# A transformer block on one core: a first pool of 160 bytes on the right side, and one padded tile

## The chip, the cores and the metric

The kernel runs on one core of a Trainium2 chip. The metric is the device time of one execution in microseconds (us); less is better. A profile of one execution stands beside the times. It names the engines PE (matrix multiply, with PEld for its weight loads), DVE (vector), ACT (scalar), POOL (GpSimd) and SP (which issues most DMAs).

## What is computed

One layer on a sequence of 1024 rows of 1024 numbers in float32: a SwiGLU feed-forward network (FFN), a mixer whose first half is attention with forget gates (8 heads) and whose second half is a gated linear recurrence (RG-LRU), and a second FFN. After each comes a layer norm over a scaled residual.

```python
x = layer_norm(DN_ALPHA * x + 0.5 * swiglu(x, ffn1_w_gate, ffn1_w_up, ffn1_w_down), ln1_g, ln1_b)
z = x @ w_in                                    # q, k, v, LRU input, LRU gate, forget logits
fox = forgetting_attention(q, k, v, fg)         # softmax(q k / 8 + cum_t - cum_s) v, causal
rec = rg_lru(causal_depthwise_conv(z_lx), ...)  # h_t = a_t h_(t-1) + b_t
mix = concat([fox, gelu(z_lg) * rec]) @ w_out
x = layer_norm(DN_ALPHA * x + mix, ln2_g, ln2_b)
x = layer_norm(DN_ALPHA * x + 0.5 * swiglu(x, ffn2_w_gate, ffn2_w_up, ffn2_w_down), ln3_g, ln3_b)

def swiglu(x, w_gate, w_up, w_down):
    return (silu(x @ w_gate) * (x @ w_up)) @ w_down      # 1024 -> 4096 -> 1024
```

## The kernel before

**Products.** Each float32 operand is split into a high part and a low part (ACT copies the high part, DVE subtracts it for the low part), and each product is three matmuls: `mm3`, lines 148 to 150, high by high, high by low, low by high. A matmul has a stationary operand (`lhs`, 128 columns, loaded into the array beforehand) and a moving one (`rhs`, up to 512 columns, streamed through). In `mm(out, lhs, rhs)` the profile prints the moving tile first: `b<-As,ws` has the moving tile `As` and the stationary tile `ws`.

**Stages.** The work runs in six stages one after the other, and PE's order is the order of the code:

1. `gate_up`, first FFN (up to about 659 us). Strassen-Winograd: each 2 by 2 block product is seven products instead of eight. There are 16 pairs of column blocks, with a gate and an up matrix each, so 32 matrices. A matrix is 7 products of 12 matmuls, 84 in all, in the order `one` (block A11), `two` (A12), `five`, `six`, `three`, `seven` (the sums s1, s2, s4, s3 of blocks), `four` (block A22). The moving tiles are the blocks of the activations; the stationary ones are the weights in the pool `gu_ws`, 16 buffers, refilled by ACT and DVE (lines 290 and 291). The profile leaves numbers out of names: `A` is A11, A12 and A22, `As` is the four sums.
2. `down_ffn`, first FFN (to about 980 us): seven products again, both operands from the pool `dn_ws`.
3. `mixer_in` (to about 1227 us): projections of the transposed rows `xT` by `w`, for each of four column groups and two halves 48 matmuls for the LRU and 48 for q and k, six small gate products of the LRU between them, and the v projection.
4. `attention` (to about 1456 us), with the output projection by `w_out` filled in between.
5. `gate_up`, second FFN (to about 2099 us).
6. `down_ffn`, second FFN (to the end).

**Where tiles lie.** A pool takes its room in SBUF when it is opened and gives it back when it is closed: one stack grows from the left (low addresses), one from the right (`side="right"`, high addresses). The address of each tile follows from the sizes of what was opened before it on its side. The left stack begins with the pool `const`. The right stack is empty until a stage opens `xl`, `dn_v`, `dn_w`, `att_qk`, `xr` or the second `gu_ws` there. All of the tiles that PE reads in lines 148 to 150 have sizes that are multiples of 256 bytes, so that a pool's place modulo 256 bytes holds for all its tiles. The tile `zx` of the LRU (line 597), 515 numbers long, is one that isn't.

Of the kernel before, what the change touches and what calls it, by code (L numbers as in the profile page):

```python
# [9 lines left out]
F32 = mybir.dt.float32  # L10
# [7 lines left out]
P = 128  # L18
# [5 lines left out]
H = 512  # L24
# [16 lines left out]
}  # L41
GELU_C = math.sqrt(2.0 / math.pi)


def f32(ap):
    return ap.bitcast(F32)


class Block:
    def __init__(self, ctx, tc):  # L50
        self.tc, self.nc, self.ctx = tc, tc.nc, ctx
        self.n = 0
        self.A, self.xT = {}, {}

        def pool(name, bufs=1, **kw):
            return ctx.enter_context(tc.tile_pool(name=name, bufs=bufs, **kw))

        self.const = pool("const")
        self.rawp = pool("rawp", 2)
        self.rowp = pool("rowp", NT)  # L60
        self.small = pool("small", 4)
        self.dram = pool("scr", 1, space=DRAM)
        nc = self.nc
        self.ident = self.const.tile([P, P], F32, name="ident")
        make_identity(nc, self.ident)
        self.eps = self.const.tile([P, 1], F32, name="eps")
        nc.vector.memset(self.eps, EPS)

    @contextmanager
    def pool(self, name, bufs=1, **kw):  # L70
        with self.tc.tile_pool(name=self.nm(name), bufs=bufs, reuse_waits="tile", **kw) as p:
            yield p
# [517 lines left out]
    def lru(self, c, half, s, tp, mix, state, between):  # L590

        nc, v = self.nc, self.nc.vector

        def tmp(tag, shape=(P, H), dt=F32):
            return tp.tile(list(shape), dt, tag=tag, name=self.nm(tag))

        zx = tp.tile([P, H + 3], F32, tag="zx", name=self.nm("zx"))
        if half == 0:
            v.memset(zx[:, 0:3], 0.0)
        else:  # L600
            v.tensor_copy(zx[:, 0:3], state["z"])
        nc.scalar.copy(zx[:, 3:], s[:, 0, :])
        if half == 0:
            state["z"] = self.small.tile([P, 3], F32, tag="zc", name=self.nm("zc"))
            v.tensor_copy(state["z"], zx[:, H:H + 3])
        u = tmp("u")
        v.tensor_scalar(u, zx[:, 3:], self.cw[:, c, 3:4], self.cb[:, c:c + 1], op0=ALU.mult, op1=ALU.add)
        for k in (2, 1, 0):
            v.scalar_tensor_tensor(u, zx[:, k:k + H], self.cw[:, c, k:k + 1], u, op0=ALU.mult, op1=ALU.add)
        uh, ul = tmp("ua", dt=F32R), tmp("ue", dt=F32R)  # L610
        nc.scalar.copy(uh, u)
        v.tensor_tensor(ul, u, f32(uh), ALU.subtract)
        g = tmp("g")
        nc.scalar.activation(g, s[:, 1, :], AF.Square)
        nc.gpsimd.tensor_scalar(g, g, 0.044715, 1.0, op0=ALU.mult, op1=ALU.add)
        v.tensor_tensor(g, g, s[:, 1, :], ALU.mult)
        nc.scalar.activation(g, g, AF.Tanh, scale=GELU_C)
        v.scalar_tensor_tensor(g, g, 1.0, s[:, 1, :], op0=ALU.add, op1=ALU.mult)
        between()
        gates = []  # L620
        for n in range(2):
            pa = self.a_tile()
            self.mm3(pa, tuple(w[:, n, :] for w in state["w"]), (uh, ul), True, True)
            gates.append(pa)
        t, tg, a, e = tmp("t"), tmp("tg"), tmp("ua"), tmp("ue")
        nc.scalar.activation(t, gates[0], AF.Tanh, bias=self.hba[:, c:c + 1], scale=0.5)
        nc.scalar.activation(tg, gates[1], AF.Tanh, bias=self.hbx[:, c:c + 1], scale=0.5)
        nc.scalar.activation(a, t, AF.Exp, bias=self.spm4[:, c:c + 1], scale=self.spm4[:, c:c + 1])
        nc.scalar.activation(t, t, AF.Tanh, bias=self.sp2[:, c:c + 1], scale=self.sp2[:, c:c + 1])
        v.tensor_scalar(a, a, 0.5, 0.5, op0=ALU.mult, op1=ALU.add)  # L630
        v.scalar_tensor_tensor(e, t, 1.0, a, op0=ALU.add, op1=ALU.mult)
        v.scalar_tensor_tensor(e, e, 2.0, a, op0=ALU.subtract, op1=ALU.mult)
        v.scalar_tensor_tensor(a, t, 1.0, e, op0=ALU.subtract, op1=ALU.mult)
        v.scalar_tensor_tensor(tg, tg, 1.0, u, op0=ALU.add, op1=ALU.mult)
        v.tensor_tensor(tg, tg, e, ALU.mult)
        nc.scalar.activation(t, t, AF.Sqrt)
        v.tensor_tensor(tg, tg, t, ALU.mult)
        v.tensor_tensor_scan(e, a, tg, 0.0 if half == 0 else state["h"], ALU.mult, ALU.add)
        if half == 0:
            state["h"] = self.small.tile([P, 1], F32, tag="hc", name=self.nm("hc"))  # L640
            v.tensor_copy(state["h"], e[:, H - 1:H])
        v.scalar_tensor_tensor(g, g, -0.5, e, op0=ALU.mult, op1=ALU.mult)
        hs = slice(half * H, (half + 1) * H)
        nc.scalar.copy(mix[0][:, hs], g)
        v.tensor_tensor(mix[1][:, hs], g, f32(mix[0][:, hs]), ALU.subtract)

    def forget(self):

        nc, v, c, z = self.nc, self.nc.vector, self.const, self.fgz
        l1p = self.log1p_exp_neg_abs(c, z, [P, HEADS, NT])  # L650
        v.scalar_tensor_tensor(z, z, 0.0, l1p, op0=ALU.min, op1=ALU.subtract)
        pre = l1p
        v.memset(pre[:, :, 0], 0.0)
        for i in range(1, NT):
            v.tensor_tensor(pre[:, :, i], pre[:, :, i - 1], z[:, :, i - 1], ALU.add)
        z, pre = (t.rearrange("p h i -> p (h i)") for t in (z, pre))
        n = HEADS * NT
        pc = self.a_tile()
        nc.tensor.matmul(pc[:, 0:n], self.tri, z, start=True, stop=False)
        nc.tensor.matmul(pc[:, 0:n], self.ones, pre, start=False, stop=True)  # L660
        v.tensor_copy(z, pc[:, 0:n])
        pt = self.a_tile()
        nc.tensor.transpose(pt[0:n, 0:P], z, self.ident)
        ct = c.tile([n, P], F32, name="ct")
        v.tensor_copy(ct, pt[0:n, 0:P])
        self.cum_d = self.dram.tile([HEADS, T], F32, name="cum_d")
        nc.sync.dma_start(self.cum_d.rearrange("h (i t) -> (h i) t", t=P), ct)
# [358 lines left out]
```

## Time and profile before

| | us |
|---|---|
| median of three runs | 2425.64 (2425.54 to 2429.72) |
| the profiled execution | 2431.77 |
| its span, first to last instruction | 2430.1 |
| PE busy in it | 2350.8 (97%) |
| DVE, ACT, POOL busy | 1816.1 (75%), 993.9 (41%), 384.3 (16%) |

The busy time of PE counts each matmul from its start to its modelled end. In a stream each starts before the one ahead has ended, so a matmul's length in the tables (some 390 ns) is more than the time from one start to the next (some 230 ns). The second is what a matmul costs in a stream; it is read from the start times of the timeline or from the count in a window. A shorter mean in a group's row goes with a shorter step.

### The profile page before, as it was taken

The page shows a single profiled execution, that of the slowest core. Times are in us where ns is not written, and L with a number is a line of the kernel's source. Part 1 is how long each engine was busy: PE and PEld are TensorE (multiplying, and loading weights), DVE is VectorE, ACT ScalarE, POOL GpSimd, SP SyncE. Part 2 cuts the span into 40 slices and gives each one's busy share as a digit, 9 for nine tenths or more (in the row PEclk, how much of TensorE's full clock was granted, in tenths as well). Part 3 has the DMA queues.
Part 4 walks back from the last instruction along what each step waited for, and adds up shares of the span by engine and source line. Part 5 has one row for each costly group of instructions (what it writes and reads, how often), then busy time and mean ns, then how long its engine had stood idle before and what let it go on. Part 6 is the DMA issues. An engine that isn't in the chain of part 4 may idle for free.

```text
span 2430.1 us, 29276 instructions
## 1 busy us (share of the span) xinstructions
PE 2350.8 (97%) x10709; PEld 1930.3 (79%) x10709; DVE 1816.1 (75%) x3059; ACT 993.9 (41%) x1748; POOL 384.3 (16%) x461
## 2 busy tenths in 40 slices
PE   7999999999999998999999898999999999999996
PEld 5888888888888887788888677888888888788885
DVE  7877777777667878866657789776777777568878
ACT  5343333333344444543546755333333333344443
POOL 2020000000010005311134442000000000010015
PEclk8999999999999999999999998999999999999998
DMA  3333232322374442332365812332323232564342
GB/s 132 112 92 113 83 113 94 118 94 102 117 258 171 154 158 70 89 105 88 105 182 142 232 53 74 109 108 88 113 83 115 97 114 98 187 222 169 129 153 87
DMA packets 175775, 298.99 MB, mean 123 GB/s; under 512 B 8128, under 2 KB 100608, under 8 KB 175632
## 3 DMA queue, kind: packets, MB, share of 16 engines
q1 hardware_dynamic: 151984, 216.06, 27.9%
q0 software_dynamic: 23648, 81.07, 8.9%
q8 instruction: 85, 1.39, 0.3%
q14 instruction: 58, 0.48, 0.1%
HBM read 214.22 MB, written 82.87 MB: 122 GB/s over the span
## 4 chain that ended last, share of the span: by engine, by line
PE 85%; DVE 9%; issue 4%; POOL 1%; DMA 1%; ACT 1%; SPq 0%; POOLq 0%; DVEq 0%; ACTq 0%
PE b L149 17%; PE b L150 17%; PE b L148 17%; PE s L150 5%; PE s L149 5%; PE s L148 5%; PE a L150 5%; PE a L149 5%; PE a L148 5%; DVE ws L461 2%; DVE row L189 1%; PE a L846 1%; PE a L830 1%; DVE st L185 1%; DMA raw<-in_ffn_w_gate_dram 1%
## 5 line engine op out<-in xcount | busy, mean ns | idle before, releaser
L148 PE MATMUL b<-As,ws 128*128 128x512 f32 x1024 | 406.2, 397 | 7.9 <-ACT As L239 7.9
L149 PE MATMUL b<-As,ws 128*128 128x512 f32 x1024 | 407.5, 398 | 4.0 <-DVE As L240 4.0
L150 PE MATMUL b<-As,ws 128*128 128x512 f32 x1024 | 408.8, 399 | 0.0
L148 PE MATMUL b<-A,ws 128*128 128x512 f32 x768 | 300.3, 391 | 4.3 <-ACT ws L290 4.3
L149 PE MATMUL b<-A,ws 128*128 128x512 f32 x768 | 300.4, 391 | 0.0
L150 PE MATMUL b<-A,ws 128*128 128x512 f32 x768 | 299.6, 390 | 0.0
L290 ACT CAST ws<-t 128x512 fp32r<-128x512 f32 x256 | 159.2, 622 | 341.9 <-PE b L149 316.4
L460 ACT CAST ws<-raw 128x512 fp32r<-128x512 f32 x224 | 139.3, 622 | 314.8 <-PE a L150 140.6
L461 DVE TENSOR_TENSOR ws<-raw,ws 128x512 fp32r<-128x512 f32 x224 | 167.2, 747 | 119.3 <-ACT ws L460 119.2
L148 PEld LDWEIGHTS b<-As,ws 128*128 128x128 f32 x1024 | 193.6, 189 | 54.6 <-ACT As L239 8.4
L149 PEld LDWEIGHTS b<-As,ws 128*128 128x128 f32 x1024 | 193.8, 189 | 53.0 <-DVE As L240 5.2
L150 PEld LDWEIGHTS b<-As,ws 128*128 128x128 f32 x1024 | 193.9, 189 | 46.3
L290 ACT CAST ws<-raw 128x512 fp32r<-128x512 f32 x192 | 118.8, 620 | 264.2 <-PE b L149 258.6
L291 DVE TENSOR_TENSOR ws<-t,ws 128x512 fp32r<-128x512 f32 x256 | 177.9, 695 | 53.6 <-ACT ws L290 53.5
L149 PE MATMUL a<-ws,ws 128*128 128x512 f32 x512 | 202.5, 395 | 7.0 <-DVE ws L461 6.9
L148 PE MATMUL a<-ws,ws 128*128 128x512 f32 x512 | 202.2, 396 | 1.4 <-ACT ws L460 1.3
L150 PE MATMUL a<-ws,ws 128*128 128x512 f32 x512 | 202.1, 395 | 0.0
L291 DVE TENSOR_TENSOR ws<-raw,ws 128x512 fp32r<-128x512 f32 x192 | 137.0, 714 | 48.9 <-ACT ws L290 48.7
L148 PEld LDWEIGHTS b<-A,ws 128*128 128x128 f32 x768 | 144.2, 188 | 35.9 <-ACT ws L290 4.7
L424 POOL DMA_DIRECT2D h_d<-row x32 | 18.6, 582 | 960.1 <-DVE row L416 927.9
L149 PEld LDWEIGHTS b<-A,ws 128*128 128x128 f32 x768 | 144.3, 188 | 31.2
L150 PEld LDWEIGHTS b<-A,ws 128*128 128x128 f32 x768 | 144.2, 188 | 30.7
(224 smaller groups left out, 4697.8 us busy)
## 6 DMA issues: line engine op xcount, KB each, us to landing
raw<-h_d SPq DMA_DIRECT2D x56, 1024.0 KB, 5.5
h_d<-row POOLq DMA_DIRECT2D x96, 512.0 KB, 3.4
raw<-in_ffn_w_gate_dram SPq DMA_DIRECT2D x32, 1024.0 KB, 5.4
raw<-in_ffn_w_up_dram SPq DMA_DIRECT2D x32, 1024.0 KB, 5.4
wd<-in_ffn_w_down_dram SPq DMA_DIRECT2D x32, 1024.0 KB, 7.7
h_d<-row POOLq DMA_DIRECT2D x32, 256.0 KB, 4.5
raw<-in_w_in_dram SPq DMA_DIRECT2D x16, 512.0 KB, 5.2
row<-in_x_dram SPq DMA_DIRECT2D x12, 512.0 KB, 7.5
```

The costliest lines, as they stand in the source:

```text
L148: mm(out, ah, bh, start=first, stop=False)
L149: mm(out, ah, bl, start=False, stop=False)
L150: mm(out, al, bh, start=False, stop=last)
L185: v.bn_stats(st[:, j, :], a[:, j * H:(j + 1) * H])
L189: v.scalar_tensor_tensor(a, a, mv[:, 0:1], gb[0], op0=ALU.subtract, op1=ALU.mult)
L290: nc.scalar.copy(hi, src)
L291: v.tensor_tensor(lo, src, f32(hi), ALU.subtract)
L424: return nc.gpsimd.dma_start(d[:, 6], s5)
L460: nc.scalar.copy(hi, src)
L461: self.mark = v.tensor_tensor(lo, src, f32(hi), ALU.subtract)
L830: nc.tensor.transpose(pa[:, (j % 4) * P:(j % 4 + 1) * P], p[:, j * P:(j + 1) * P], self.ident)
L846: mm(pv[:, ps], vt[:, j, :], pts[h, qt][j // 4][l][:, j % 4, ps], start=j == 0 and l == 0, stop=j == last and l == 1)
```

## The change

A pool `edge` is opened first on the right side with one tile of 40 numbers (160 bytes) for each partition. No instruction touches it. All that is later opened on the right side lies 160 bytes lower. The tile `zx` is 576 numbers long instead of 515, of which 515 are used, so that what follows it in its pool and the pools after it start elsewhere. The tile `ct` of `forget` is no more; its values go into the first 64 partitions of `ones`, which was read for the last time by a product a few lines earlier. So `const` is 512 bytes smaller, and all that follows on the left lies 512 bytes lower.

```diff
+LINE = 64
+EDGE = 40
...
+        self.edge = pool("edge", side="right")
+        self.edge.tile([P, EDGE], F32, name="edge")
         self.const = pool("const")
...
-        zx = tp.tile([P, H + 3], F32, tag="zx", name=self.nm("zx"))
+        zx = tp.tile([P, H + LINE], F32, tag="zx", name=self.nm("zx"))[:, 0:H + 3]
...
-        ct = c.tile([n, P], F32, name="ct")
+        ct = self.ones[0:n]
         v.tensor_copy(ct, pt[0:n, 0:P])
```

Every engine issues the same instructions with the same shapes in the same order. The addresses that the program gives to the two operands, modulo 256 bytes:

| matmuls | count | moving, stationary before | moving, stationary after |
|---|---|---|---|
| `gate_up` 1, sums `As` (right) by `ws` | 1536 | 224, 64 | 64, 64 |
| `gate_up` 1, blocks A11, A12, A22 by `ws` | 1152 | 64, 64 | 64, 64 |
| `down_ffn` 1 and 2, `ws` by `ws` | 2688 | 64, 64 | 64, 64 |
| `mixer_in`, `xT` (right) by `w` | 768 | 224, 64 | 64, 64 |
| `mixer_in`, LRU gates, `ua`, `ue` by the gate weights | 48 | 96, 96 | 64, 64 |
| `mixer_in`, v: `wv` (0, 64, 128, 192 past 64) by `xT` | 384 | mixed, 224 | mixed, 64 |
| attention, `kh`, `kl` by `q` (all right) | 192 | 224, 224 | 64, 64 |
| attention, `pt` by `v` (right) | 320 | 64, 224 | 64, 64 |
| output projection, `w` by `mix` | 384 | 64, 64 | 64, 64 |
| `gate_up` 2, sums `As` (left) by `ws` (right) | 1536 | 64, 224 | 64, 64 |
| `gate_up` 2, blocks A11, A12, A22 by `ws` (all right) | 1152 | 224, 224 | 64, 64 |

The transposes (`ident` by a tile, line 234 and line 830) have 128 and 64 before and after.

One wait of the second `down_ffn` moves with the addresses: the DMA that loads its first `wd` tile no longer waits for PE, and the next `wd` load, two issues later on SP, does.

## The prediction

> **What bounds the kernel now.** I read the page first, then a table of windows by stage, then the list of waits, then single starts in the timeline.
>
> ```profile
> span 2430.1 us, 29276 instructions
> PE 2350.8 (97%) x10709; PEld 1930.3 (79%) x10709; DVE 1816.1 (75%) x3059; ACT 993.9 (41%) x1748; POOL 384.3 (16%) x461
> PE 85%; DVE 9%; issue 4%; POOL 1%; DMA 1%; ACT 1%; SPq 0%; POOLq 0%; DVEq 0%; ACTq 0%
> ```
>
> PE is busy for 97% of the span, and the chain that ended last runs over PE for 85% of it. A shorter matmul therefore shortens the end, as long as the matmul stands in a stretch where PE doesn't wait. The table of windows tells which stretches those are (the columns are the window, its length, busy time of PE, PEld, DVE, ACT and POOL with counts, PE's granted clock, DMA share and GB/s):
>
> ```profile
> 100.00:640.00 540.00, 540.00 (x2334) 438.54 (x2333) 395.61 (x643) 184.51 (x308) 48.33 (x73) 1.00 0.30 101
> ...
> 740.00:900.00 160.00, 160.00 (x708) 132.48 (x707) 133.60 (x209) 67.17 (x118) 6.30 (x5) 1.00 0.48 170
> ...
> 1010.00:1230.00 220.00, 217.94 (x1116) 183.62 (x1116) 138.45 (x256) 103.41 (x166) 39.13 (x60) 1.00 0.35 109
> 1230.00:1440.00 210.00, 193.78 (x1136) 164.65 (x1136) 161.05 (x415) 133.38 (x299) 89.85 (x146) 0.98 0.56 153
> ...
> 1500.00:2080.00 580.00, 580.00 (x2506) 471.01 (x2505) 427.89 (x679) 197.41 (x330) 42.34 (x61) 1.00 0.30 101
> ```
>
> In both `gate_up` stages (the first and the last row) PE is busy without a break, at the full granted clock, with DVE at 73% and 74%. In `mixer_in` it misses 2 of 220 us, in attention 16 of 210. The same rows give what a matmul costs: 540 us / 2334 = 231.4 ns in the first `gate_up`, but 160 us / 708 = 226.0 ns in `down_ffn`, although both consist of matmuls of one shape at one clock. The groups by line show where the difference is (after the bar: busy us, mean ns of one, idle us):
>
> ```profile
> L150 PE MATMUL b<-As,ws 128*128 128x512 f32 x1024 | 408.8, 399 | 0.0
> L150 PE MATMUL b<-A,ws 128*128 128x512 f32 x768 | 299.6, 390 | 0.0
> L150 PE MATMUL s<-ws,ws 128*128 128x512 f32 x384 | 149.4, 389 | 0.0
> L150 PE MATMUL s<-xT,w 128*128 128x512 f32 x256 | 101.5, 397 | 0.0
> ```
>
> Two groups are at 389 to 390 ns and two at 397 to 399. Set beside the table of addresses in the section on the change, the longer ones (`As`, `xT`) are those whose two operands differ modulo 256 bytes, and the shorter ones (`A`, `ws` by `ws`) those where they agree. The step from start to start is measured in the timeline (start, length, engine, line). First one matrix of the first `gate_up`, then one of the second, then `down_ffn`, then `mixer_in`:
>
> ```profile
> 461.83 0.39 PE L148 MATMUL b<-A,ws 128*128 128x512 f32 x1
> ...
> 463.92 0.39 PE L148 MATMUL b<-A,ws 128*128 128x512 f32 x1
> ...
> 464.60 0.39 PE L148 MATMUL b<-A,ws 128*128 128x512 f32 x1
> ...
> 470.04 0.40 PE L148 MATMUL b<-As,ws 128*128 128x512 f32 x1
> ...
> 481.28 0.39 PE L148 MATMUL b<-A,ws 128*128 128x512 f32 x1
> ...
> 1804.97 0.40 PE L148 MATMUL b<-A,ws 128*128 128x512 f32 x1
> ...
> 1813.17 0.40 PE L148 MATMUL b<-As,ws 128*128 128x512 f32 x1
> ...
> 1824.39 0.40 PE L148 MATMUL b<-A,ws 128*128 128x512 f32 x1
> ...
> 2199.66 0.39 PE L148 MATMUL a<-ws,ws 128*128 128x512 f32 x1
> ...
> 2219.38 0.39 PE L148 MATMUL a<-ws,ws 128*128 128x512 f32 x1
> ...
> 1036.22 0.40 PE L150 MATMUL a<-ua,lo 128*128 128x512 f32 x1
> ...
> 1058.95 0.40 PE L148 MATMUL a<-ua,hi 128*128 128x512 f32 x1
> ```
>
> - 464.60 to 470.04 are the products `one` and `two` (A11, A12), 24 matmuls: 5.44 / 24 = 226.7 ns.
> - 470.04 to 481.28 are the four products on sums, 48 matmuls: 11.24 / 48 = 234.2 ns. In the second `gate_up` 1813.17 to 1824.39: 11.22 / 48 = 233.8 ns. There the sums lie on the left and `ws` on the right, the other way round from the first, and the blocks A11, A12 and A22 lie on the right beside `ws`. So neither the side nor the distance sorts the groups; the difference modulo 256 does.
> - 2199.66 to 2219.38 is `ws` by `ws`, 87 steps: 226.7 ns, with both operands in a third pool.
> - 1036.22 to 1058.95 holds one gate matmul and 96 of `xT`: 22.73 / 97 = 234.3 ns.
> - 461.83 to 464.60 is `four` (A22), 12 matmuls: 2.77 / 12 = 230.8 ns, though its operands agree. The first nine take 2.09 us (232 ns each), the last three 0.68 us (227 ns). I read this as a lag that the stretch before leaves behind and that dies out within nine matmuls; the 24 after it show nothing of it.
>
> [...]
>
> **The sum.** No instruction is added, removed or moved, so the sum has the step alone.
>
> - `gate_up`, first FFN: a matrix now takes 481.28 - 461.83 = 19.45 us for its 84 matmuls. With all operands at 64 it should take 84 x 0.2267 = 19.04 us (the A22 lag goes too, because nothing before it differs). 0.41 us x 32 matrices = 13.1 us.
> - `gate_up`, second FFN: 1824.39 - 1804.97 = 19.42 us, 0.38 us x 32 = 12.2 us.
> - `mixer_in`: 768 matmuls on `xT` x (234.3 - 226.7) = 5.8 us.
> - `down_ffn`, output projection: operands agree before and after. Nothing.
> - Attention: `pt` by `v` comes to agree. I have no such matmul with equal places to price it by. If its step shrank by the same share (7.5 of 234.2, 3.2%), the group below would give at most 3.2% of 41.7 us, 1.3 us; if other work sets the pace there, as the 16 us that PE misses suggest, nothing. The v projection in `mixer_in` has three of four places still unequal. I take nothing, and keep 0 to 1.5 us for the range.
>
> ```profile
> L846 PE MATMUL a<-pt,v 128*128 128x256 f32 x256 | 41.7, 297 | 1.1 <-DVE pt L835 0.9
> ```
>
> What could hold the gain back in `gate_up` is the making of weights. The waits say who is ahead (waiting instruction, what it waited for, total us, times, longest us):
>
> ```profile
> ACT ws L290 <- PE b L149: 575.1, 349, 2.2
> ```
>
> ACT waits 575 us in all for PE to release a `ws` buffer: the weights are ready a full pool ahead, and a PE that is 2% faster only shortens these waits. DVE would go from 73% to 75%. Nor do DVE and ACT depend on where tiles lie: the same subtraction costs as much with `ws` at 64 (window 100 to 640) as with `ws` at 224 (window 1510 to 2080).
>
> ```profile
> L291 DVE TENSOR_TENSOR ws<-t,ws 128x512 fp32r<-128x512 f32 x111 | 76.0, 685 | 24.6 <-ACT ws L290 24.6
> L291 DVE TENSOR_TENSOR ws<-t,ws 128x512 fp32r<-128x512 f32 x118 | 80.8, 685 | 27.0 <-ACT ws L290 27.0
> ```
>
> The other edits cost nothing. `edge` is never touched; `zx` is read and written over the same 515 numbers; the copy into `ones` comes after a product and a transpose for which it waits anyway. The `wd` load that takes over the wait for PE is two issues behind the one that had it, so SP is free of it earlier, not later; if its cover is gone, it costs at most one landing once.
>
> Sum: 13.1 + 12.2 + 5.8 = 31.1 us. The profiled execution, 2431.77 us with a span of 2430.1, would come to 2400.7; it is 6.1 us over the median of the runs, from which I subtract: 2425.6 - 31.1 = 2394.5 us. The difference that a measurement here can tell from none is about 0.2%, 4.9 us.
>
> **Rivals.**
>
> - *Agreement alone isn't enough.* The equal products of A22 stand at 230.8 ns, not at 226.7. If that is their own pace and no lag, because something besides the remainder counts, then the sums may come down only to 230.8. Then 3072 matmuls gain 3.4 or 3.0 ns and `xT` 768 x 3.5 ns: 9.8 + 2.7 = 12.5 us, 2413 us. For it: the A22 rows. Against it: the last three of twelve are at 227.
> - *The change does nothing.* The sums and `xT` take longer for another reason that goes with these tiles, and 31 us stay: 2425.6 us. For it: only two tiles take longer, and the trace itself doesn't show the places. [...] Against it: the sums change sides between the FFNs and stay at 234, and A22 in the same stage and of the same shape settles.
> - *Equal places collide.* The remainder counts the other way: two streams that start at one remainder ask for the same thing at the same time, and something else, such as the order in which pools were filled, makes A11, A12 and `ws` quicker. A22 would then show the price of equality, 230.8 - 226.7 = 4.1 ns, to be added to the 3840 matmuls that come to agree: 15.7 us, 2441 us. It decides from the point where a sum takes over 234.2 ns in the new layout. Against it: 226.7 ns in three pools with equal places.
>
> **How the numbers follow.** The full gain has 0.78: five places agree with it and none of the 227 ns groups contradicts. The partial gain has 0.10, no effect 0.08, collision 0.04. Faster by over 0.2% holds the first two, 0.88; within it 0.08; slower 0.04. The full gain alone would be 2390 to 2399: 1.5 us more from attention and, since the shown runs are up to 4.1 us apart, about 3 us to either side. To cover a gain that is partly lost, most of the way to the partial rival, the range goes from 2389 to 2411.
>
> **What would show it right or wrong.** In the profile after, the groups `b<-As,ws` and `s<-xT,w` should have the 389 to 390 ns of the others; 48 products on sums should take 10.9 us, a block of 84 should take 19.04, and A22 should be at 227 from its first matmul. A window of 540 us in `gate_up` should hold some 2380 matmuls instead of 2334, still busy without a break, and ACT's 575 us of waiting for PE should shrink by about the 25 us. If the groups stay at 397 to 399, the remainder isn't the cause; if they fall but the span doesn't follow, another engine has become late, and `ws` L290 or L291 would then stand as what PE waits for. A lasting pace over 227 in all would speak for the partial rival.

## The result, and the profile after

| | before | after |
|---|---|---|
| median of the runs, us | 2425.8 (2425.54 to 2429.72) | 2396.19 (2391.57 to 2396.48) |
| the profiled execution, us | 2431.77 | 2396.48 |
| its span, us | 2430.1 | 2394.8 |

The ratio is 0.987, with a 95% interval from 0.9853 to 0.9887: 29.6 us less by the medians, where 31.1 were forecast. Both kernels, measured once more later, gave 2396.51 (2393.51 to 2397.09) against 2427.15 for the kernel before, ratio 0.9868 (0.9853 to 0.9883). One run of the experiment with the right side at 0 took 2530.62 us at a granted clock of 0.88, where its others had 0.986 to 0.988, and is not among that experiment's numbers below.

The head of the page of the kernel after: the instruction counts of every engine are those of before, and only PE has become shorter by more than 3 us, by 2350.8 - 2318.7 = 32.1 us.

```profile
span 2394.8 us, 29276 instructions
PE 2318.7 (97%) x10709; PEld 1927.6 (80%) x10709; DVE 1814.8 (76%) x3059; ACT 993.3 (41%) x1748; POOL 383.0 (16%) x461
PE 85%; DVE 8%; issue 3%; DMA 1%; ACT 1%; POOL 1%; SPq 0%; POOLq 0%; DVEq 0%; ACTq 0%
```

Its table of windows, one row for the first `gate_up` with the window of the prediction, and one for the second (columns as in the prediction):

```profile
100.00:640.00 540.00, 540.00 (x2384) 447.15 (x2383) 398.25 (x647) 186.96 (x313) 48.69 (x73) 1.00 0.30 103
...
1500.00:2060.00 560.00, 560.00 (x2472) 463.88 (x2471) 408.39 (x648) 192.77 (x323) 39.10 (x58) 1.00 0.31 107
```

PE is still busy without a break, with 2384 matmuls in the 540 us that held 2334 before: 226.5 ns each. The groups by line (`mm3` is at lines 153 to 155 now):

```profile
L155 PE MATMUL b<-As,ws 128*128 128x512 f32 x1024 | 400.3, 391 | 0.0
L155 PE MATMUL b<-A,ws 128*128 128x512 f32 x768 | 299.0, 389 | 0.0
L155 PE MATMUL s<-ws,ws 128*128 128x512 f32 x384 | 149.4, 389 | 0.0
L155 PE MATMUL s<-xT,w 128*128 128x512 f32 x256 | 100.2, 391 | 0.0
...
L851 PE MATMUL a<-pt,v 128*128 128x256 f32 x256 | 41.0, 294 | 1.1 <-DVE pt L840 0.9
```

`As` fell from 399 to 391 ns and `xT` from 397 to 391. `A` and `ws` by `ws`, whose operands agreed before, stayed within 1 ns. The timeline of the kernel after, at the rows where the moving tile changes, in the first `gate_up`, then the second, then `mixer_in` (start, length, engine, line):

```profile
442.49 0.39 PE L153 MATMUL b<-As,ws 128*128 128x512 f32 x1
...
453.37 0.39 PE L153 MATMUL b<-A,ws 128*128 128x512 f32 x1
...
456.08 0.39 PE L153 MATMUL b<-A,ws 128*128 128x512 f32 x1
...
461.52 0.39 PE L153 MATMUL b<-As,ws 128*128 128x512 f32 x1
...
1783.78 0.39 PE L153 MATMUL b<-As,ws 128*128 128x512 f32 x1
...
1794.66 0.39 PE L153 MATMUL b<-A,ws 128*128 128x512 f32 x1
...
1802.82 0.39 PE L153 MATMUL b<-As,ws 128*128 128x512 f32 x1
...
1023.67 0.39 PE L153 MATMUL s<-xT,w 128*128 128x512 f32 x1
...
1045.43 0.39 PE L153 MATMUL a<-ua,hi 128*128 128x512 f32 x1
```

The 48 products on sums take 453.37 - 442.49 = 10.88 us in the first FFN and 10.88 in the second (11.24 and 11.22 before). A block of 84 takes 461.52 - 442.49 = 19.03 us (19.45 before). The 12 of A22, from 453.37 to 456.08, take 2.71 us, 226 ns each. The 96 of `xT` take 21.76 us, 226.7 ns each.

Since one execution of the kernel before ran 3.7 us longer than another, the stages are set out for two profiled executions of each kernel (second pair: the same addresses, profiled again). A stage goes from its first matmul to the first one of the next, read from the start times (the 17 to 18 us ahead of the first matmul are left out):

| us | before | before again | after | after again | forecast |
|---|---|---|---|---|---|
| `gate_up` 1 | 641.30 | 641.60 | 628.95 | 629.11 | -13.1 |
| `down_ffn` 1 | 322.64 | 322.64 | 322.61 | 322.61 | 0 |
| `mixer_in` | 256.30 | 258.40 | 251.11 | 251.58 | -5.8 |
| attention | 217.83 | 214.16 | 212.93 | 212.05 | 0 to -1.5 |
| `gate_up` 2 | 643.10 | 641.10 | 630.81 | 631.11 | -12.2 |
| `down_ffn` 2 and the end | 331.13 | 331.07 | 330.83 | 330.89 | 0 |
| span | 2430.1 | 2426.4 | 2394.8 | 2394.6 | -31.1 |

The two spans of before differ by 3.7 us, and attention alone differs by as much (217.83 and 214.16). So the 35.3 us between the first two profiles is more than the change brings; the second pair differs by 31.8.

### The profile page after: what moved, and what is told of

Its sections match the earlier page's. It is cut to its first block, busy times and chain, and to the rows that moved or that the text cites. A ratio compares the mean times of both kernels' runs of the same rounds, so it can differ in the third digit from the quotient of the medians.

```text
span 2394.8 us, 29276 instructions
## 1 busy us (share of the span) xinstructions
PE 2318.7 (97%) x10709; PEld 1927.6 (80%) x10709; DVE 1814.8 (76%) x3059; ACT 993.3 (41%) x1748; POOL 383.0 (16%) x461
## 4 chain that ended last, share of the span: by engine, by line
PE 85%; DVE 8%; issue 3%; DMA 1%; ACT 1%; POOL 1%; SPq 0%; POOLq 0%; DVEq 0%; ACTq 0%
PE b L154 17%; PE b L155 17%; PE b L153 17%; PE s L155 5%; PE s L154 5%; PE s L153 5%; PE a L155 5%; PE a L154 5%; PE a L153 5%; DVE ws L466 2%; DVE row L194 2%; PE a L851 1%; DMA raw<-in_ffn_w_gate_dram 1%; DVE st L190 1%; PE a L835 1%
## 5 line engine op out<-in xcount | busy, mean ns | idle before, releaser
L153 PE MATMUL b<-As,ws 128*128 128x512 f32 x1024 | 400.7, 392 | 8.2 <-ACT As L244 8.2
L154 PE MATMUL b<-As,ws 128*128 128x512 f32 x1024 | 400.7, 391 | 3.8 <-DVE As L245 3.8
L155 PE MATMUL b<-As,ws 128*128 128x512 f32 x1024 | 400.3, 391 | 0.0
```

The source lines that it names most:

```text
L153: mm(out, ah, bh, start=first, stop=False)
L154: mm(out, ah, bl, start=False, stop=False)
L155: mm(out, al, bh, start=False, stop=last)
```

## The experiments

The theory: in a stream of 512-column matmuls of this kernel, the step from start to start depends on where the two operands lie modulo 256 bytes; equal places give 226.7 ns, others more. Its rivals: the time comes from something else in the new layout (the padded `zx`, the shorter `const`, another order of tiles); or one particular place is good, and the operands needn't agree; or two streams merely mustn't start close to each other.

### The other two edits alone

The pool `edge` is left out, and the padded `zx` and the reuse of `ones` stay. The right side is back at 224.

```diff
-        self.edge = pool("edge", side="right")
-        self.edge.tile([P, EDGE], F32, name="edge")
```

> The change without the pool on the right: zx padded and ct put into ones, so the left side lies 512 bytes lower and the right side where it was. Theory 'difference modulo 256': As and xT still differ by 160 or 96 bytes, the time stays at that of before, 2425.6 us (within 3 us), As at 234 ns a step. Rival 'the smaller const pool or the new place on the left brings it': 2396 us.

Measured: 2427.53 us (2426.3 to 2433.15) against 2427.56 (2423.2 to 2433.49), ratio 1.0 (0.9991 to 1.0009). The groups by line are those of before:

```profile
L153 PE MATMUL b<-As,ws 128*128 128x512 f32 x1024 | 408.1, 399 | 0.0
...
L153 PE MATMUL b<-A,ws 128*128 128x512 f32 x768 | 299.9, 390 | 0.0
...
L153 PE MATMUL s<-xT,w 128*128 128x512 f32 x256 | 101.8, 398 | 0.0
```

From start to start the sums of the first `gate_up` take 234.2 ns and `xT` 234.2, as before. The whole gain hangs on the 160 bytes. That is still no proof of agreement: every tile on the right moved with them.

### The right side at 192: it moves, but doesn't agree

```diff
-EDGE = 40
+EDGE = 72
```

288 bytes instead of 160: the right side lies at 192, the left at 64, and the two differ by 128.

> The pool on the right has 288 bytes instead of 160: the right side lies at 192, the left at 64, a difference of 128 everywhere. Theory 'difference modulo 256': As and xT take 231 to 238 ns a step and the time is that of before, 2420 to 2430 us. Rival 'modulo 128 or 64 is enough': 2396 us. Rival 'any shift of the right side does it': 2396 us.

Measured: 2422.54 us (2419.05 to 2427.99), ratio 0.998 (0.997 to 0.9991). From the groups by line:

```profile
L155 PE MATMUL b<-As,ws 128*128 128x512 f32 x1024 | 406.4, 397 | 0.0
...
L155 PE MATMUL s<-xT,w 128*128 128x512 f32 x256 | 101.7, 397 | 0.0
```

The steps of `As` and `xT` are 233.2 to 233.5 ns, and A22 behind them is at 228 in place of 230 to 231. A pool ahead of all others on the right is thus worth almost nothing as long as the places differ: 5 us of the 31. The steps account for that: a block of 84 takes 19.37 us in both FFNs (19.45 and 19.41 before), and `xT` 1.0 ns less, 0.08 x 32 + 0.04 x 32 + 0.8 = 4.6 us.

### Both sides at 128: they agree, elsewhere

```diff
-EDGE = 40
+EDGE = 24
...
+        self.lead = pool("lead")
+        self.lead.tile([P, 16], F32, name="lead")
         self.const = pool("const")
```

> Both sides moved once more: 64 bytes on the left, 96 on the right, so that both operands lie at 128. Theory 'difference modulo 256': as the changed kernel, 2396 us (within 3 us), all groups at 227 ns a step. Rival 'the place 64 itself is what counts': As, xT and also A and ws by ws move away from 227, 2426 us or more.

Measured: 2396.58 us (2395.47 to 2400.59), ratio 0.9874 (0.9861 to 0.9888). From the groups by line:

```profile
L157 PE MATMUL b<-As,ws 128*128 128x512 f32 x1024 | 400.8, 391 | 0.0
...
L157 PE MATMUL s<-xT,w 128*128 128x512 f32 x256 | 100.2, 391 | 0.0
```

The steps of `As`, `A` and `xT` are at 226.7 ns again. The particular place 64 has no part in it; the rival of one good place falls.

### The right side at 0: the sign of the difference

```diff
-EDGE = 40
+EDGE = 56
```

The right side lies at 0, the left at 64. Moving less stationary is then 192 (modulo 256) in the first `gate_up` and for `xT`, and 64 in the second `gate_up`, where the sums lie on the left.

> The pool on the right has 224 bytes: the right side lies at 0, the left at 64. In the first gate_up and in mixer_in the moving operand then lies 192 bytes past the stationary one, in the second gate_up 64 bytes. Theory 'the step follows the difference with its sign, as the step kernel gave it': 233.3 ns for As in the first gate_up and for xT, 229 ns for As in the second; against before some 1.4 us less in the first, 0.8 in mixer_in, 7 and about 1 for A22 in the second: 2427.6 - 10 = 2417 us. Rival 'any difference costs alike': 2427 us (within 3). Rival 'multiples of 64 are free': 2396 us.

Measured: 2413.5 us in the median of four runs (2411.7 to 2414.51) against 2427.15, ratio 0.994 (0.9926 to 0.9954). The table of windows has the two `gate_up` stages:

```profile
100.00:630.00 530.00, 530.00 (x2298) 430.20 (x2298) 391.15 (x637) 181.56 (x304) 48.33 (x73) 1.00 0.30 103
1500.00:2060.00 560.00, 560.00 (x2450) 459.66 (x2449) 415.06 (x660) 193.00 (x323) 40.88 (x60) 1.00 0.30 104
```

One and the same distance of 64 bytes costs 530 / 2298 = 230.6 ns in the mean where the moving operand is the lower one, and 560 / 2450 = 228.6 ns where it is the higher one. The products on sums stand at 233.3 and 228.9. So the difference has a sign, and the steps of the sums are those that the expectation had from signed differences. Its time is not: 2417 us were expected, 3.5 more. The steps give 9.4 us (a block of 84 takes 19.38 us in the first FFN and 19.21 in the second, 19.45 and 19.41 before, and `xT` gains 0.8 us), and A22 in the second stays at 231 ns, where 1 us less was expected. What the other 4 of the 13.7 us between the medians are is not shown.

### The step by itself, in a kernel that does nothing else

A kernel that computes nothing of the block: after a few loads and copies it issues groups of matmuls back to back on two tiles, `st` (stationary) and `mv` (moving), with a start that differs from group to group. One group:

```python
b = bank()  # moving 32 bytes past the stationary, 512 columns
for i in range(144):
    mm(b, sl(st, 0, i % 4, 128), sl(mv, 32, i % 4, 512), start=i == 0, stop=i == 143)
```

Between unequal groups stands a group with equal places. The differences are the multiples of 32, with 256, 4 and 16; behind them come two groups whose matmuls alternate, then 256 and 128 columns, and bf16. In this kernel and the two like it below, a place is counted from the start of the tile, and the program puts `mv` and `st` 128 bytes past a multiple of 256. Differences and remainders by 32 are not touched by that; a place called 0 is 128 in the count of the block's kernel. `mv` and `st` are declared float32r, as the block's split operands are; the profile prints f32. No stream of plain float32 operands was run.

> This kernel computes nothing of the block: it streams groups of 144 matmuls, each group at one pair of places of the moving and the stationary operand, and stores the sums. Theory 'difference modulo 256': groups with difference 0 and 256 bytes take 227 ns a step, those with 32 to 224 bytes 231 to 238 ns, those with 4 and 16 bytes more than 227 too. Rival 'smaller grain' (only the difference modulo 64 or 128 counts): 64, 128 and 192, or 128 alone, stand at 227 too. Rival 'something of the big kernel' (pools, other engines): all groups of 512 columns are alike. Of the two mixed groups, if the weights being loaded during a matmul (those of the next one) are what collides, 'own equal, next differs' takes 234 and 'own differs, next equal' 227; if the matmul's own weights count, the other way round. For 256 and 128 columns and for bfloat16 no figure is known; the theory expects difference 0 to be the least in each.

The groups by line, one line for each group: difference 0, 32, 64, 128, 160, 256, 4, and the last one bf16 with difference 0:

```profile
L63 PE MATMUL b<-mv,st 128*128 128x512 f32 x144 | 32.8, 389 | 0.0
...
L67 PE MATMUL b<-mv,st 128*128 128x512 f32 x144 | 33.8, 395 | 0.0
...
L71 PE MATMUL b<-mv,st 128*128 128x512 f32 x144 | 33.1, 391 | 0.0
...
L79 PE MATMUL b<-mv,st 128*128 128x512 f32 x144 | 33.8, 395 | 0.0
...
L83 PE MATMUL b<-mv,st 128*128 128x512 f32 x144 | 33.9, 396 | 0.0
...
L95 PE MATMUL b<-mv,st 128*128 128x512 f32 x144 | 32.8, 389 | 0.0
...
L103 PE MATMUL b<-mv,st 128*128 128x512 f32 x144 | 34.3, 399 | 0.0
...
L151 PE MATMUL b<-mb,sb 128*128 128x512 bf16 x144 | 31.3, 379 | 0.0
```

The step follows from such a row: busy time less one length, over the steps between, (32.8 - 0.389) / 143 = 226.6 ns for equal places and (33.8 - 0.395) / 143 = 233.6 ns for a difference of 32. From the start times, without the first twelve of a group: 226.7 at 0 and at 256; 233.3 at 32, 228.9 at 64, 233.4 at 96, 233.4 at 128, 234.3 at 160, 233.3 at 192 and at 224; 236.7 at 4 and 231.6 at 16. At the same granted clock of 1.0 and with hardly any other engine at work, the 160 of the kernel before gives the 234.3 ns of its timeline, and 64 and 192 those of the experiment before this one. Equal groups that follow an unequal one settle at 226.7 within 4 to 10 matmuls: that is A22's lag. So 64, 128 and 192 are not free, which the rival 'smaller grain' asked for, and the groups are not alike, which the other rival asked for.

Of the alternating groups, the one whose own places agree and whose next weights lie 96 bytes off took 234.0 ns, and the one whose own places differ and whose next weights agree took 230.0, in turns of 224 and 236. The expectation had 227 for one of the two. It also had difference 0 as the least for every width, and that failed: 256 columns took 120.0 ns at 0 and at 96 but 117.4 at 160, and 128 columns took 111.7 at 0 and at 96.

bf16 takes 215.8 ns at 0, 96 and 160 alike: at these three differences the place doesn't matter. The float32r groups of this kernel at their best, 226.7 ns, stand 11 ns above it.

### Every multiple of 4, and which of two matmuls matters

The same kind of kernel, 72 matmuls a group, difference 0, 4, 8 and so on to 252; then 256 columns; then two groups in which only one of the operands alternates between 0 and 96; then groups with both operands at 96, 4, 16 and 128.

> Computes nothing of the block; streams as in the first step kernel, with the moving operand 0, 4, 8, ... 252 bytes past the stationary one for 512 columns, every 16 bytes for 256 columns, then mixed groups. Theory 'difference modulo 256, any difference costs': only 0 is at 227 ns, all others lie at 231 to 238, and 64, which stood at 229, is the only dip. Rival 'a smooth curve': the step grows and shrinks with the distance, with a dip around 64 and neighbours of 0 (4, 252) near 227. Group A (moving always at 0, stationary at 0 and 96 in turn): if the weights loaded during a matmul, those of the next one, are what counts, matmuls whose next weights lie at 0 take 227 and the others 234; if their own, the other way round; the mean is 230 either way. Group B (moving at 0 and 96 in turn, stationary at 0): the matmuls at 0 take 227, those at 96 take 234. Both operands at 96, at 4, at 16 and at 128: all at 227 if only the difference counts.

The groups by line, for the differences 0 and 20, and below them the groups with both operands at 96 and at 4:

```profile
L63 PE MATMUL b<-mv,st 128*128 128x512 f32 x72 | 16.5, 389 | 0.0
...
L83 PE MATMUL b<-mv,st 128*128 128x512 f32 x72 | 17.4, 404 | 0.0
...
L407 PE MATMUL b<-mv,st 128*128 128x512 f32 x96 | 22.0, 390 | 0.0
...
L411 PE MATMUL b<-mv,st 128*128 128x512 f32 x96 | 23.1, 401 | 0.0
```

Of 64 differences only 0 gives 226.7 ns. The others lie between 228.9 (64) and 240 (20, 36, 68 and others). The rival of a smooth curve falls: 4 bytes cost 10 ns, 252 bytes 3.4. Three things came out otherwise than expected. The others do not all lie at 231 to 238 with 64 as the only dip: 60 gives 229.2, 236 gives 229.4, and several stand at 230.0 or at 240. The groups with one alternating operand gave 230.0 ns both, in turns of 229 and 231, so that it can't be read from them whether a matmul's own weights or the next one's collide with its moving operand. And both operands at 4 gave 239.2 ns, both at 16 gave 230.0, although they agree. Agreement alone isn't enough after all.

### Equal places, over all places

Both operands at the same place, 0, 4, 8 and so on to 252; then 256 columns with other pairs of places; then alternating groups by other differences.

> Computes nothing of the block; both operands at the same place, 0, 4, 8, ... 252 bytes past a multiple of 256, for 512 columns; then 256 columns at some pairs; then the two mixed groups at 32, 64, 128 and 160 bytes. Theory 'equal places are enough': all 64 groups at 227 ns. Rival 'equal and a multiple of 32 bytes' (96 and 128 stood at 227, 4 at 239 and 16 at 230): the eight groups at multiples of 32 at 227, the others at 229 to 240, no matter that the places are equal. For 256 columns at difference 192 (moving 64, stationary 128; moving 0, stationary 64) 113 ns, at 0 120. Mixed groups: if the weights of the next matmul count, C (own equal, next differs) stands at 233 and D (own differs, next equal) at 227; if both count, C and D lie between, as they did at 96 bytes (C 234, D 230).

The groups by line, both operands at 0, 4, 16 and 32:

```profile
L63 PE MATMUL b<-mv,st 128*128 128x512 f32 x72 | 16.5, 389 | 0.0
...
L67 PE MATMUL b<-mv,st 128*128 128x512 f32 x72 | 17.4, 401 | 0.0
...
L79 PE MATMUL b<-mv,st 128*128 128x512 f32 x72 | 16.8, 393 | 0.0
...
L95 PE MATMUL b<-mv,st 128*128 128x512 f32 x72 | 16.5, 389 | 0.0
```

226.7 ns stands at the eight multiples of 32 and nowhere else: 239.1 at 4 and 36, 232.7 at 8 and 40, 230.0 at 12 and 44, 231.1 at 16 and 48, 236.7 at 20 and 24, 233.4 at 28, and so on with a period of 32. Over the pairs that were run, 512 columns therefore took 226.7 ns where two things held: equal modulo 256, and a multiple of 32. The kernel before had the second and lacked the first, which is why the prediction's reading of it came out whole. The prediction asked for agreement alone; that 64 is also a multiple of 32 was luck.

The prices of unequal or odd places are less firm than the 226.7. The same pair of places took 233.4 ns in the first step kernel and 232.5 in the second (128 bytes apart), and 230.0 in the second and 231.1 here (both at 16). In such groups the single steps fall into a repeating pattern, and one pair of places has more than one pattern: at 128 bytes, 238 and 229 ns in turn in the first kernel, a longer one from 228 to 241 in the second.

With 256 columns it is otherwise. Equal places at multiples of 32 give 120.0 ns, at 16 and 48 118.4; moving at 64 with stationary at 128 or at 0 gives 113.3; moving at 64 with stationary at 224 gives 120.0; moving at 0 with stationary at 64 gives 117.8, where 113 was expected from the difference. In the second step kernel the differences 112 and 192 gave 113.3, and the other fourteen 116.7 to 120.0. One of these is the very pair of 64 and 0, and there it took 117.8 ns. The second kernel's group first, then this one's:

```profile
L339 PE MATMUL b<-mv,st 128*128 128x256 f32 x96 | 11.5, 279 | 0.0
```

```profile
L359 PE MATMUL b<-mv,st 128*128 128x256 f32 x96 | 11.0, 276 | 0.0
```

So at 256 columns the places alone don't set the step, and I have no rule for it.

The alternating groups leave the same question open as before. With matmuls whose own places agree and whose next weights differ, the step is 231.7 ns for 32, 231.7 for 64, 228.3 for 128 and 234.0 for 160; with own places that differ and next weights that agree it is 233.4, 233.3, 230.0 and 230.1. Neither is free, and neither is the whole price. The block's kernel before the change shows what is loaded when. First two matmuls, then the weight load of the second of them:

```profile
461.60 0.40 PE L150 MATMUL b<-As,ws 128*128 128x512 f32 x1
461.83 0.39 PE L148 MATMUL b<-A,ws 128*128 128x512 f32 x1
```

```profile
461.60 0.19 PEld L148 LDWEIGHTS b<-A,ws 128*128 128x128 f32 x1
```

By these records the load that runs from one start to the next is that of the next matmul's weights. It isn't longer where the places differ: between 100 and 640 us of that kernel the mean load is 188 ns for `As` by `ws` (224 and 64) and 188 for `A` by `ws` (64 and 64), at steps of 234.2 and 226.7. If only the next weights counted, though, the second kind of group would take 226.7 ns.

### Attention by the 256-column prices

By those prices `pt` (64) by `v` should be quicker with `v` at 128; in the count of the step kernels that is the pair 192 and 0, at 113.3 ns. A tile of 96 bytes is put behind `v` in its pool, on top of the change; nothing touches it:

```diff
+                qkp.tile([P, 24], F32, tag="gap", name=self.nm("gap"))
```

> The changed kernel with 96 bytes (twice) after v in the attention's pool: v lies at 128, pt at 64, so pt is 192 bytes past v; q, kh and kl lie at 128 all three; the rest as in the changed kernel. By the step kernel a matmul of 256 columns takes 113 ns at this difference instead of 119 to 120 at equal places: 256 x 6 ns = 1.5 us less than the changed kernel where PE sets the pace, nothing where it does not; ratio to before 0.9865 against 0.987, not to be told apart by the time alone. Rival 'equal is best there too': the step of pt by v grows from 119 ns, and the time by up to 1.5 us.

Measured: 2400.19 us (2398.09 to 2403.59) against 2428.01 (2424.72 to 2432.41) for the kernel before, ratio 0.9883 (0.9864 to 0.9903): no gain over the change, whose interval in a run of its own is 0.9853 to 0.9883. The group by line fell by 0.3 us against the 41.0 of the kernel after:

```profile
L852 PE MATMUL a<-pt,v 128*128 128x256 f32 x256 | 40.7, 293 | 1.1 <-DVE pt L841 0.9
```

The step within the stream fell from 118.9 to 116.5 ns, not to 113, which for 256 matmuls is 0.6 us at most, while attention as a stage took 220.39 us in place of 212.93. In its chain that ended last, a load of `cum` stands at the head of attention, where the chain of the kernel after has only issue, time without a wait that the profile shows; first the kernel after, then this one:

```profile
1216.53 6.39 issue
...
1224.76 0.96 DVE p L821
```

```profile
1215.05 8.99 DMA cum<-cum_d
...
1227.63 0.96 DVE p L822
```

The first `p` of the attention weights comes 2.9 us later. The lengths of attention wander by as much without any edit there (217.83 and 214.16 for one program), so I take from this only that the 0.6 us can't be seen in the end, not that the gap does harm. That stays open: its four runs (from 2398.09 us) all lie above the eight of the kernel after (up to 2397.09), which were measured at other times.

### The pair again

The kernels before and after once more, with no edit, to see how far a pair of profiles can be trusted.

> The changed kernel once more, beside more runs of the kernel before. 31 us less than before, ratio 0.9872; the spans of its profiled execution and of the kernel before may differ by more or less than that (35 us in the first pair). If the 4 us over 31 belong to the change, attention (last two heads) is again some 4 us shorter than in the kernel before; if they are chance, it is not.

> The kernel before once more, for a second profile of the same program: stages up to attention within 1 us of the first profile. If the length of the last two heads of attention is chance, it differs from the first profile's 71 us by a few us; if it goes with the places, it is the same within 1 us.

Measured: 2396.51 us for the kernel after, with a span of 2394.6, and 2428.11 us for the kernel before, with a span of 2426.4; the stages stand in the table above. The terms of `gate_up` 1 and of both `down_ffn` repeat within 0.3 us, that of `gate_up` 2 within 2.3 us (12.3 and 10.0) and that of `mixer_in` within 1.6 (5.2 and 6.8), that of attention doesn't (4.9 and 2.1). The expectation that the kernel before repeats within 1 us up to attention failed in `mixer_in`, 256.30 and 258.40 us.

## Why the prediction was right

Step by step, as the prediction put them:

- **PE bounds, and a shorter step shortens the end.** Held. Over the whole first `gate_up`, the same DVE work (759 instructions) and the same number of matmuls, to two, stand in a window that is 13 us shorter. First the row of before, then that of after:

```profile
18.00:659.00 641.00, 634.36 (x2752) 515.48 (x2753) 474.29 (x759) 231.38 (x391) 63.09 (x85) 0.99 0.30 100
```

```profile
18.00:646.00 628.00, 621.34 (x2750) 514.42 (x2749) 473.25 (x759) 230.83 (x391) 63.44 (x85) 0.99 0.30 102
```

- **The place modulo 256 sorts the groups.** Held, and now shown from both sides: undoing the 160 bytes takes all of it back (2427.53 us against 2427.56), another common place gives it again (2396.58 us with both at 128), and a kernel of matmuls alone has the same steps (226.7 and 234.3 ns at differences of 0 and 160). With hardly any other engine at work, the float32r groups took 226.7 to 240 ns by place, the bf16 groups 215.8 ns at each of three differences. That the weight load is what disturbs the stream is not shown, since no run here has a stream without loads; shown is that the step goes with the places of the two operands.
- **A22's 230.8 ns is a lag.** Held: 226 ns behind equal sums, and in the kernel of matmuls alone a lag of 4 to 10 matmuls. The rival "Agreement alone isn't enough" was built on this row and falls for this kernel. In its own words it is true elsewhere: both operands at 4 take 239 ns. The prediction's table of places, all multiples of 32, had no case that could show it.
- **The terms.** `gate_up` 1 gave 12.4 and 12.5 us of the 13.1, `gate_up` 2 gave 12.3 and 10.0 of the 12.2, `mixer_in` 5.2 and 6.8 of the 5.8. The sum of these three is 29.8 and 29.3 us where 31.1 were forecast, and 29.6 and 30.6 us by the medians of the runs. In the step itself nothing is missing. Most of each `gate_up` is 28 blocks of 84 one behind the other; they take 19.45 us each before and 19.04 after in the first stage, 11.4 us for the 28, and 19.41 and 19.04 in the second, 10.4 us, and both pairs of profiles agree on that. What the prediction sized too large is the count of 32: the other four matrices gave 1.0 and 1.1 us in the first stage, where 1.6 were counted. At its start PE waits for its operands and runs at a granted clock of 0.87, and a shorter step doesn't show there: 170 matmuls stand in the first 42 us before and after.

```profile
18.00:60.00 42.00, 35.36 (x170) 29.15 (x171) 38.82 (x54) 25.49 (x46) 11.87 (x8) 0.87 0.14 44
```

```profile
18.00:60.00 42.00, 35.34 (x170) 29.35 (x169) 38.57 (x54) 25.23 (x46) 11.99 (x8) 0.87 0.15 43
```

In the second stage the rest is 1.8 us in one pair and -0.5 in the other; there the two executions of the kernel before differ by 2.0 us.
- **Attention.** Taken as nothing, and that is what the parts give: `pt` by `v` went from 119.3 to 118.9 ns, 0.1 us for 256. The 4.9 and 2.1 us of the stage are no answer to the change that I could show, since 3.7 of them stand between two executions of the kernel before.
- **The weights stay ahead.** Held. ACT's wait for PE fell by 575.1 - 548.8 = 26.3 us, about 25 forecast, and DVE's share of the first `gate_up` rose from 474.29 / 641 = 74.0% to 473.25 / 628 = 75.4%. The waits of the kernel after:

```profile
ACT ws L295 <- PE b L154: 548.8, 321, 2.1
```

- **The other edits cost nothing.** Held: 0.0 us without `edge`, in an interval of 2.2 us to either side. The wait of the `wd` load that moved shows in no stage, 331.13 and 330.83 us in the last.
- **"Equal places collide"** falls at its own point: a sum takes 226.7 ns, not over 234.2.

## What to carry to other kernels

Where a long stream of equal matmuls has two steps in one trace, at one clock and with no wait, print the addresses of both operands beside the groups before looking for a cause among the engines. In float32r products of 512 columns, as made here, put both operands at one place modulo 256 bytes and at a multiple of 32: a stream that keeps to such a place took 226.7 ns a step, one at another fixed pair that was run 228.9 to 240; it costs one untouched tile and gave 1.3% here. For other widths and types measure a stream first: 256 columns (113.3 to 120.0 ns) and bf16 (215.8 at three differences) did not follow this. Size such a gain by the matmuls that come to agree times the step between the two kinds of groups, and set a profiled pair of executions against its own scatter before giving a stage credit for the rest.

## What the runs showed that I had not expected

- The 32-byte grain: two operands that agree at 4 bytes past a multiple of 32 take 239 ns, more than the 234 ns of the kernel before.
- The difference has a sign: the moving operand 64 bytes above the stationary one costs 2.2 ns, 64 below it 6.6 ns.
- 256 columns were quickest at some places that do not agree (113.3 ns against 120.0), and one and the same pair of places gave 113.3 in one kernel and 117.8 in another.
- bf16 showed none of this: 215.8 ns at each of three differences.
- What stays open is the mechanism. Matmuls whose own places agree took 228.3 to 234.0 ns among neighbours whose weights differ, and matmuls whose own places differ took 230.0 to 233.4 where the next weights agree; the alternating groups don't part the two, and the trace only shows that each load runs during the matmul ahead of its own (from 461.60 us, where the matmul it belongs to starts at 461.83).
